# Tables of a state-space mixer with fewer instructions, B and C for eight groups at a time, phases by twos, and all pieces spread over the first feed forward

## The chip, the cores and the metric

The kernel runs on one core of a Trainium2 chip. The metric is the device time of one launch in microseconds (us); the median over runs is given. Engines are PE (TensorE, with its weight loads PEld), DVE (VectorE), ACT (ScalarE), POOL (GpSimd) and SP (SyncE, which here only issues DMAs). Each engine executes its instructions in the order in which they stand in its queue.

## The reference

A decoder trunk of two layers on x (1, 1024, 1024) in f32. Each layer is a mixer, a feed forward of squared ReLU (1024 to 4096 to 1024), and a gated per-layer embedding (PLE). Layer 0 mixes with RWKV-7 plus a short convolution, layer 1 with S5, a diagonal complex state space of 64 groups, with 16 channels and 64 states in each.

```python
def s5_mixer(hn, lambda_re, lambda_im, log_step, b_re, b_im, c_re, c_im, d_skip, glu_w1, glu_w2):
    u = hn.reshape(bsz, t, 64, 16)
    lam = complex(minimum(lambda_re, -1e-4), lambda_im)          # (64 groups, 64 states)
    step = exp(log_step)[:, None]
    lam_bar = exp(lam * step)
    b_bar = ((lam_bar - 1.0) / lam)[..., None] * complex(b_re, b_im)
    ...                                   # h[t] = lam_bar * h[t-1] + b_bar u[t];  y = Re(c h)
    y = gelu(y + d_skip * u)
    return (y @ glu_w1) * sigmoid(y @ glu_w2)

for i in range(2):
    h = h + mix_fns[i](rms_norm(h, norm_mix[i]), *mix_params[i])
    h = h + square(relu(rms_norm(h, norm_ffn[i]) @ ffn_up[i])) @ ffn_down[i]
    h = h + (p[i] @ ple_proj[i]) * sigmoid(rms_norm(h, norm_ple[i]) @ ple_gate[i])
return rms_norm(h, norm_final)
```

What the S5 mixer needs besides u depends on the parameters alone: powers of lam_bar, b_bar, its products with B and C, phases. None of it depends on x.

## The kernel before

The program runs through the mixer of layer 0, feed forward 0 (FFN0), PLE 0, S5 with its gated linear unit, feed forward 1 (FFN1), PLE 1 and the final norm. Every f32 product is made of three matmuls of a high and a low part (hi by hi, lo by hi, hi by lo: lines L159 to L161 in `mm3`).

**Feed forward** (`ffn`). A loop over k runs from -6 to 62; each k has 8 steps. In one k, PE executes 24 matmuls of the up projection into ps_up and 21 of the down projection, in seven groups of three into the three PSUM tiles ps_dnx, ps_dny and ps_dnz (L354); X is used by four of the seven. After each group, DVE adds the tile to h or ha (L357, "eviction"), and the next group on the same tile waits for that. The order of PE is written by hand (`manual_schedule`), and the table `due` says at which step an instruction of another engine, or of a piece, is emitted: `at(k, s, f)`. The order on the other engines is the scheduler's. For each k, DVE also makes r_up (L311, from PSUM), hidl (L319, the low part of an activation), a difference (L325) and the low part of the down weights wlo (L283); POOL makes the low part of the up weights (L260) and sums of down weights (L273 to L276), a quarter of the hidl and of the differences too. FFN0 and FFN1 execute the same matmuls of their own; only FFN0 has S5 work beside it.

The row norm for the feed forward comes through acc (POOL, L198, sums of squares), ps_ms (PE, L215), a reciprocal (DVE, L219) and ps_rs (PE, L225); L177 makes prl, the low part of the input of the up projection (16 of DVE).

**S5 work in FFN0.** `s5_tables` makes the tables of lam_bar by power series, on [128, 64] tiles on DVE (helpers `mul` L890, `add` L893, `sub` L896, `aff` L899). They are emitted before FFN0, and stand on DVE from 702 to about 900 us. After that come the pieces, one for 2 of the 64 groups, and the phases of a piece:

```python
S5_AT, S5_EACH, S5_FFN = 74, 8, 30
S5_STEPS = (0, 7, 8, 9, 10, 12, 13, 16, 18, 19), (9, 11, 13, 15, 17, 20)
for n, gs in enumerate(pieces(t5, range(S5_FFN))):
    for g, steps in zip(gs, S5_STEPS):
        for s in steps:
            at(0, S5_AT + S5_EACH * n + s, lambda g=g: next(g, 0))
```

So 30 of the 32 pieces begin at step 74 (k = 9) and follow each other by 8 steps, one in each k; the two others, with their phases, are woven into PLE 0. A piece (`s5_piece`) loads C and B of its 2 groups, turns C on PE (ps_c, L1049), scales it on DVE (cx, L1052), makes b_bar on DVE (u L1059, w L1060, o L1061, twice), CL on POOL (L1068 to L1071), BL on DVE (L1078, L1079, L1081), turns it on PE (ps_bl, L1087), makes the kernel block on PE (ps_k, L1095), and adds the skip block on POOL (L1099). `s5_phases` doubles a [128, 2, 128] table of phases in 7 steps, with two scalings on ACT and two operations on POOL (L1120, L1121) in a step.

**The end of mixer 0** (`mixer0_run`) is ordered by `MIX_JOBS`, one string for each chain of the recurrence; a job of `Wabc` is a part of the output projection (ps_wo) that fills PE while the chain waits. W45b, W67b read ybh and ybl (the convolution's half), W2b and W3b read yah and yal (the recurrence's half). `R` is the last step of the recurrence's read-out, `C6` and `C7` are steps of the convolution.

Of the kernel before, what the change touches and what calls it, by code (L numbers as in the profile page):

```python
# [5 lines left out]
F32 = mybir.dt.float32  # L6
# [6 lines left out]
P = 128  # L13
# [6 lines left out]
S5_AT, S5_EACH, S5_FFN = 74, 8, 30  # L20
S5_STEPS = (0, 7, 8, 9, 10, 12, 13, 16, 18, 19), (9, 11, 13, 15, 17, 20)
# [10 lines left out]
MIX_JOBS = ['z1 C0', 'z2 C1 W45a', 'z3 C2 X3', 'N M L z4 W01a', 'z5 C4', 'z6 W23a', 'z7 C5 S', 'W45b R C6', 'W01b C7', 'W67b W2b W3b', '']  # L32
# [25 lines left out]
class Trunk:  # L58
# [822 lines left out]
    def s5_tables(self, pool, sp, keep_p):  # L881
        nc, i = self.nc, self.i
        V = nc.vector
        n = [0]

        def t(nm="t"):
            return pool.tile([P, 64], F32, tag="s5t", name=nm, bufs=14)

        def mul(a, b):
            o = t(); V.tensor_mul(o, a, b); return o  # L890

        def add(a, b):
# [15 lines left out]
        def keep(a, nm, where=None):  # L908
            o = (where or pool).tile([P, 64], F32, name=nm); V.tensor_copy(o, a); return o

        def doub(E):
            return mul(E, aff(E, 1.0, 2.0))

        exp_c = [1.0 / m for m in range(2, 11)]

        def em1(x):
            return mul(horner(x, exp_c), x)

        def lam(nm):
# [7 lines left out]
        lre = pool.tile([P, 64], F32, name="lre")
        V.tensor_scalar_min(lre, lam("l1_lambda_re"), -1e-4)
        lim = pool.tile([P, 64], F32, name="lim")
        V.tensor_copy(lim, lam("l1_lambda_im"))  # L930
        ls = t("ls")
        nc.sync.dma_start(ls, i["l1_log_step"].rearrange("(o g) -> o g", o=1).broadcast_to([P, 64]))
        x = t("lsc")
        V.tensor_scalar(x, ls, -100.0, 1.0 / 128, ALU.max, ALU.mult)
        E = em1(x)
        for _ in range(4):
            E = doub(E)
        E = aff(E, 1.0, 1.0)
        for _ in range(3):
            E = mul(E, E)  # L940
        step = keep(E, "step")

        x = mul(lre, step)
        x2 = t("x2")
        V.tensor_scalar(x2, x, -80.0, 1.0 / 128, ALU.max, ALU.mult)
        E = em1(x2)
        for _ in range(7):
            E = doub(E)
        em = keep(E, "em")

        y = mul(lim, step)
        a = t("rnd")
        V.tensor_scalar(a, y, 1.0 / (2 * math.pi), 12582912.0, ALU.mult, ALU.add)
        nn = aff(a, 1.0, -12582912.0)
# [42 lines left out]
        m = mag  # L997
        for _ in range(3):
            m = mul(m, m)
        self.rho = keep_p.tile([P, 32], F32, name="rho")  # L1000
        for g in range(NG):
            V.tensor_copy(self.rho[64 * g:64 * g + 64], m.rearrange("p (q g) -> p g q", g=NG)[64 * g:64 * g + 64, g])

        raw = pool.tile([64, P], F32, tag="lraw", name="lraw", bufs=1)
        nc.sync.dma_start(raw.rearrange("g (r c) -> g r c", c=16),
                          i["l1_d_skip"].rearrange("(g o c) -> g o c", o=1, c=16).broadcast_to([64, 8, 16]))
        ps = self.pm.tile([P, H], F32, tag="m", name="ps_lam")
        nc.tensor.transpose(ps[:, 0:64], raw, self.ident[0:64, 0:64])
        eye = pool.tile([P, 16], F32, name="eye")
        V.tensor_reduce(eye, self.ident.rearrange("p (r c) -> p c r", c=16), mybir.AxisListType.X, ALU.add)  # L1010
        self.skip = sp.tile([P, 64, 16], F32, name="skip")
        V.tensor_copy(self.skip, ps[:, 0:64].rearrange("p (g o) -> p g o", o=1).broadcast_to([P, 64, 16]))
        V.tensor_mul(self.skip, self.skip, eye.rearrange("p (o c) -> p o c", o=1).broadcast_to([P, 64, 16]))


        r, im = cosy, siny
        self.wk = sp.tile([P, 7, 2, 32], F32, name="wk")
        for k in range(10):
            if k >= 3:
# [625 lines left out]
```

## Time and profile before

| | us |
|---|---|
| median of 3 runs (2765.99 to 2766.64) | 2766.43 |
| the profiled execution, its own time | 2769.96 |
| span of the profiled execution | 2768.2 |
| mixer 0, until 740.0 | 740.0 |
| FFN0, 740.0 to 1533.9 | 793.9 |
| PLE 0, 1533.9 to 1657.4 | 123.5 |
| FFN1, 1952.7 to 2628.6 | 675.9 |
| PLE 1, 2628.6 to 2751.8 | 123.2 |

The span is the time from the first to the last instruction; the profiled execution has 1.8 us around it, and is 3.5 us above the median. Times within the program are us from the start of the span. PE is busy for 94% of the span, DVE for 70%; the clock columns give the TensorE clock that was granted, as a share of 2.4 GHz.

### The profile page before, as it was taken

To read this page: it belongs to the slowest core of one execution; us is meant where nothing else is said; L and a number is where in the kernel's file an instruction comes from. 1 tells how busy PE (TensorE), PEld (TensorE's weight loads), DVE (VectorE), ACT (ScalarE), POOL (GpSimd) and SP (SyncE) were. 2 spreads that over 40 slices of the span, in tenths; PEclk is the share of its full clock that TensorE was granted. 3 is DMA by queue.
4 is the path that set the end of the run, shared out by engine and by line. 5 is a ranking of instruction groups with operands and counts; after the bars stand their busy time and mean duration, and the time that the engine had idled before them with its cause. 6 is when DMAs were issued, how large, how long until landed. Compare 5 with 4: busy or idle time off the path is not lost.

```text
span 2768.2 us, 48385 instructions
## 1 busy us (share of the span) xinstructions
PE 2601.9 (94%) x18829; PEld 2079.1 (75%) x18829; DVE 1928.5 (70%) x2992; ACT 1087.9 (39%) x2075; POOL 1178.5 (43%) x1771
## 2 busy tenths in 40 slices
PE   7999999989898889998999997899999999999998
PEld 5777777768676667777788786788788888888777
DVE  6655666563799888888777748622577777777854
ACT  4334444343432454444553525512433233233432
POOL 4434433443343577677663505511343433433410
PEclk9999999999899999999999998999999999999999
DMA  4213311321211233333211315311111111111121
GB/s 104 62 55 101 93 55 48 107 72 51 71 50 42 75 86 90 90 97 84 65 60 50 89 44 157 106 53 45 36 54 47 53 54 46 54 54 46 50 76 61
DMA packets 273441, 189.16 MB, mean 68 GB/s; under 512 B 36110, under 2 KB 255484, under 8 KB 273212
## 3 DMA queue, kind: packets, MB, share of 16 engines
q1 hardware_dynamic: 249232, 158.26, 19.5%
q10 hardware_dynamic: 21084, 19.17, 2.7%
q0 software_dynamic: 2896, 8.65, 0.9%
q8 instruction: 148, 2.42, 0.4%
q14 instruction: 81, 0.66, 0.1%
HBM read 156.92 MB, written 29.10 MB: 67 GB/s over the span
## 4 chain that ended last, share of the span: by engine, by line
PE 66%; DVE 14%; POOL 8%; issue 5%; DMA 3%; ACT 3%; SPq 0%; ACTq 0%; POOLq 0%; DVEq 0%
PE ps_dnx L354 9%; PE ps_up L161 6%; PE ps_up L159 6%; PE ps_up L160 6%; PE ps_dny L354 4%; PE ps_z L159 3%; PE ps_z L160 3%; PE ps_z L161 3%; PE ps_gl L159 2%; PE ps_gl L161 2%; PE ps_gl L160 2%; DVE ha L357 2%; PE ps_dnz L354 2%; PE ps_g L159 2%; PE ps_g L160 2%
## 5 line engine op out<-in xcount | busy, mean ns | idle before, releaser
L159 PE MATMUL ps_up<-prh,uwh 128*128 128x512 f32 x1024 | 407.6, 398 | 3.6 <-ACT uwh L257 3.6
L161 PE MATMUL ps_up<-prh,uwl 128*128 128x512 f32 x1024 | 408.5, 399 | 2.1 <-POOL uwl L260 2.1
L160 PE MATMUL ps_up<-prl,uwh 128*128 128x512 f32 x1024 | 406.0, 396 | 0.0
L260 POOL TENSOR_TENSOR uwl<-uraw,uwh 128x512 fp32r<-128x512 f32 x136 | 182.3, 1341 | 172.1 <-ACT uwh L257 171.2
L354 PE MATMUL ps_dnx<-hidh,whi 128*128 128x512 f32 x480 | 199.3, 415 | 46.4 <-DVE ha L357 46.1
L159 PEld LDWEIGHTS ps_up<-prh,uwh 128*128 128x128 f32 x1024 | 195.4, 191 | 49.5 <-ACT uwh L257 4.0
L161 PEld LDWEIGHTS ps_up<-prh,uwl 128*128 128x128 f32 x1024 | 194.9, 190 | 47.7 <-POOL uwl L260 2.6
L273 POOL TENSOR_TENSOR draw<-draw 128x128 f32<-128x128 f32 x120 | 65.3, 544 | 387.2 <-DMA draw<-in_l_ffn_down_dram 329.2
L160 PEld LDWEIGHTS ps_up<-prl,uwh 128*128 128x128 f32 x1024 | 195.1, 191 | 45.3
L148 POOL TENSOR_TENSOR wlo<-wraw,whi 128x1024 fp32r<-128x1024 f32 x66 | 159.6, 2420 | 141.7 <-ACT whi L147 129.2
L357 DVE TENSOR_TENSOR h<-h,ps_dnx 128x512 f32<-128x512 f32 x240 | 164.0, 683 | 57.5 <-PE ps_dnx L354 56.6
L198 POOL TENSOR_TENSOR acc<-acc,sq 128x512 f32<-128x512 f32 x70 | 104.8, 1505 | 215.3 <-ACT sq L197 214.5
L354 PE MATMUL ps_dnx<-hidl,whi 128*128 128x512 f32 x480 | 190.2, 396 | 4.5 <-DVE hidl L319 4.5
L354 PE MATMUL ps_dnx<-hidh,wlo 128*128 128x512 f32 x480 | 190.1, 396 | 0.0
L147 ACT CAST whi<-wraw 128x1024 fp32r<-128x1024 f32 x104 | 108.7, 1048 | 196.4 <-PE ps_z L160 73.2
L319 DVE TENSOR_TENSOR hidl<-r_up,hidh 128x512 fp32r<-128x512 f32 x188 | 158.8, 856 | 37.3 <-ACT r_up L315 30.8
L257 ACT CAST uwh<-uraw 128x512 fp32r<-128x512 f32 x136 | 84.0, 619 | 247.1 <-PE ps_up L160 234.0
L357 DVE TENSOR_TENSOR ha<-ha,ps_dnx 128x512 f32<-128x512 f32 x240 | 163.3, 680 | 18.4 <-PE ps_dnx L354 18.4
L159 PE MATMUL ps_z<-prh,whi 128*128 128x512 f32 x416 | 175.8, 423 | 0.1
L161 PE MATMUL ps_z<-prh,wlo 128*128 128x512 f32 x416 | 164.2, 395 | 1.7 <-POOL wlo L148 1.7
L160 PE MATMUL ps_z<-prl,whi 128*128 128x512 f32 x416 | 164.8, 396 | 0.6 <-DVE prl L480 0.6
L314 ACT ACTIVATE hidh<-r_up 128x512 fp32r<-128x512 f32 x98 | 61.7, 630 | 235.8 <-DVE r_up L311 228.9
(441 smaller groups left out, 6611.4 us busy)
## 6 DMA issues: line engine op xcount, KB each, us to landing
uraw<-in_l_ffn_up_dram SPq DMA_DIRECT2D x128, 256.0 KB
draw<-in_l_ffn_down_dram SPq DMA_DIRECT2D x120, 256.0 KB
wraw<-in_l_w_in_dram SPq DMA_DIRECT2D x52, 512.0 KB
s5w<-s5w SPq DMA_DIRECT2D x32, 384.0 KB
wraw<-in_l_w_out_dram SPq DMA_DIRECT2D x16, 512.0 KB
wraw<-in_l_ple_gate_dram SPq DMA_DIRECT2D x16, 512.0 KB
wraw<-in_l_glu_w_dram SPq DMA_DIRECT2D x16, 512.0 KB
toep<-kt ACTq DMA_DIRECT2D x32, 240.0 KB
```

The lines of the kernel that those rows point to most:

```text
L147: nc.scalar.copy(hi[:, :n], raw[:, :n])
L148: self.lo_engine().tensor_sub(lo[:, :n], raw[:, :n], hi[:, :n].bitcast(F32))
L159: nc.tensor.matmul(ps, wh, xh, start=start, stop=False)
L160: nc.tensor.matmul(ps, wh, xl, start=False, stop=False)
L161: nc.tensor.matmul(ps, wl, xh, start=False, stop=stop)
L198: (eng or nc.vector).tensor_add(acc, acc, sq)
L257: A.copy(uw[m][0], raws["u"])
L260: nc.gpsimd.tensor_sub(uw[m][1], raws["u"], uw[m][0].bitcast(F32))
L273: G.tensor_add(raw[:, 4], raw[:, 0], raw[:, 2])
L319: return lambda: eng.tensor_sub(st[nm][1], t, st[nm][0].bitcast(F32))
L354: nc.tensor.matmul(ps, w[:, a], v, start=id(ps) not in begun, stop=n == 2, skip_group_check=True)
L357: V.tensor_add(hv, hv, ps)
```

## The change

1. `s5_tables`: constants are folded into one instruction `(o + c) * x` (`series`) in place of a multiply and an affine one, tiles are written in place, powers of lam_bar are doubled (1, 2, 4 at a time) in place of one by one, and the phase factors wk lie in one tile `lv` and are copied by 2 instructions in place of 14. The 1024-wide skip table is gone: only its diagonal source dT and the mask eye16 are kept. DVE instructions of the tables: 272 before, 141 after. All loads of raw parameters are issued at the start. It is a generator now, called twice in each step from step -38 (in k = -5) on.
2. `s5_front` is new: loads, turns and scalings of B and C for 8 groups at once (8 fronts in place of 32 parts of pieces). The scaling of C moves from DVE to ACT; the skip product is made here on POOL, for 8 groups.
3. `s5_piece` keeps the rest: CL, BL, turn, kernel block.
4. `s5_phases` makes two pieces' phases in one call: the POOL instructions are half as many and twice as wide, the ACT instructions are as many as before.
5. The 32 pieces follow each other by 14 steps from step 36 to the end of FFN0; none is left for PLE 0.
6. `MIX_JOBS`: `W45b R C6` becomes `R C6 W45b`, `W67b W2b W3b` becomes `W2b W67b W3b`.

Lines from `s5_tables` on have other numbers in the changed kernel; those before it have 3 more.

```diff
-S5_AT, S5_EACH, S5_FFN = 74, 8, 30
-S5_STEPS = (0, 7, 8, 9, 10, 12, 13, 16, 18, 19), (9, 11, 13, 15, 17, 20)
+S5_START, S5_PREP, S5_AT, S5_EACH = -38, 2, 36, 14
+S5_FRONT = (-20, -6, -4, -3)
+S5_STEPS = (0, 2, 4, 7, 10)
+S5_PH = (1, 5, 9, 13, 17, 21, 25)
...
-MIX_JOBS = ['z1 C0', 'z2 C1 W45a', 'z3 C2 X3', 'N M L z4 W01a', 'z5 C4', 'z6 W23a', 'z7 C5 S', 'W45b R C6', 'W01b C7', 'W67b W2b W3b', '']
+MIX_JOBS = ['z1 C0', 'z2 C1 W45a', 'z3 C2 X3', 'N M L z4 W01a', 'z5 C4', 'z6 W23a', 'z7 C5 S', 'R C6 W45b', 'W01b C7', 'W2b W67b W3b', '']
...
-        def horner(x, coef):
-
-            p = aff(x, coef[-1], 1.0)
-            for c in reversed(coef[:-1]):
-                p = aff(mul(p, x), c, 1.0)
-            return p
...
+        def series(o, x, coef):
+
+            V.tensor_scalar_mul(o, x, float(coef[-1]))
+            for n, c in enumerate(reversed(coef[:-1])):
+                stt(o, o, float(c), x, ADD)
+                if n % 2:
+                    yield
...
-        for k in range(1, 8):
-            r, im, r1, i1 = self.LR[:, :, k], self.LI[:, :, k], self.LR[:, :, 1], self.LI[:, :, 1]
-            V.tensor_sub(self.LR[:, :, k + 1], mul(r, r1), mul(im, i1))
-            V.tensor_add(self.LI[:, :, k + 1], mul(r, i1), mul(im, r1))
...
+        for n in (1, 2, 4):
+            a, b = (q[:, :, 0:n] for q in tt)
+            lo, hi = slice(1, n + 1), slice(n + 1, 2 * n + 1)
+            rn, im = (q[:, :, n:n + 1].broadcast_to([P, 64, n]) for q in (R, I))
+            V.tensor_mul(a, R[:, :, lo], rn)
+            V.tensor_mul(b, I[:, :, lo], im)
+            yield
...
+    def s5_front(self, n, pool):
+        gs = slice(8 * n, 8 * n + 8)
...
+        ps = self.pm.tile([P, H], F32, tag="m", name="ps_c")
+        for m, raw in enumerate(raws):
+            nc.tensor.transpose(ps[:, m * P:(m + 1) * P], raw, self.ident)
+        X = pool.tile([P, 2, 8, 16], F32, tag="cx", name="cx", bufs=1)
+        nc.scalar.activation(X.rearrange("p n g c -> p (n g c)"), ps[:, 0:2 * P], AF.Copy, scale=self.nsgn)
+        yield
+        bc = lambda a: a.rearrange("p (g o) -> p g o", o=1).broadcast_to([P, 8, 16])
...
+        for m in range(2):
+            V.tensor_mul(Bb[:, m], Bs[m], bc(self.Fr[:, gs]))
+            V.tensor_mul(w, Bs[1 - m], bc(self.Fi[:, m, gs]))
+            V.tensor_add(Bb[:, m], Bb[:, m], w)
...
+            for j in range(2):
+                for o, n in ((E[:, j, :, m:2 * m], 0), (t[:, j, :, :m], 1)):
+                    nc.scalar.activation(o, E[:, j, :, 0:m], AF.Copy, scale=self.wk[:, k, n, pc + j:pc + j + 1])
+            G.tensor_sub(E[:, :, 0, m:2 * m], E[:, :, 0, m:2 * m], t[:, :, 1, :m])
+            G.tensor_add(E[:, :, 1, m:2 * m], E[:, :, 1, m:2 * m], t[:, :, 0, :m])
...
+                            def start(s):
+                                for _ in range(S5_PREP):
+                                    if next(tab, self) is self:
+                                        return
+                                at(0, s + 1, lambda: start(s + 1))
+                            at(0, S5_START, lambda: start(S5_START))
+                            for n in range(64 // NG):
+                                s0 = S5_AT + S5_EACH * n
+                                gs = [(lazy(self.s5_piece, n), S5_STEPS)]
...
-                            side = pieces(t5, range(S5_FFN, 64 // NG))
-                        self.ple(l, st2["xn"], rstd, pt, done1, [q for a, b in side for q in [a] * 4 + [b] + [a, b] * 5 + [a]])
+                        self.ple(l, st2["xn"], rstd, pt, done1, [])
```

**PE, the end of mixer 0.** These are rows of PE behind the last step of the recurrence (ps_z is a last part of the input projection, ps_yt turns the recurrence's result). Before, the 48 ybh and ybl matmuls come first:

```order
L161 MATMUL ps_z<-prh,wlo 128x512
L159 MATMUL ps_wo<-ybh,whi 128x512
L160 MATMUL ps_wo<-ybl,whi 128x512
L161 MATMUL ps_wo<-ybh,wlo 128x512
L159 MATMUL ps_wo<-ybh,whi 128x512
...
L799 MATMUL ps_yt<-ident,Y 128x128 x4
L159 MATMUL ps_wo<-yah,whi 128x512
```

After, 24 matmuls of the other half stand at this place, and ybh only behind them:

```order
L164 MATMUL ps_z<-prh,wlo 128x512
L162 MATMUL ps_wo<-yah,whi 128x512
L163 MATMUL ps_wo<-yal,whi 128x512
L164 MATMUL ps_wo<-yah,wlo 128x512
...
L162 MATMUL ps_wo<-ybh,whi 128x512
L163 MATMUL ps_wo<-ybl,whi 128x512
...
L802 MATMUL ps_yt<-ident,Y 128x128 x4
L162 MATMUL ps_wo<-ybh,whi 128x512
```

So 24 matmuls that read earlier results moved ahead of the first ones that need the second half of ybh; as many of the ybh ones moved behind ps_yt.

**PE, the start of FFN0.** These rows are those around ps_ms and ps_rs, through which the row norm passes. Before, 28 matmuls of ps_up stand ahead of ps_ms and 21 between it and ps_rs:

```order
L159 MATMUL ps_up<-prh,uwh 128x512
L215 MATMUL ps_ms<-meanw,acc 128x1 x4
L160 MATMUL ps_up<-prl,uwh 128x512
L161 MATMUL ps_up<-prh,uwl 128x512
...
L159 MATMUL ps_up<-prh,uwh 128x512
L225 MATMUL ps_rs<-ident,rs_8946 128x128 x4
L924 MATMUL ps_lam<-ident,lraw 128x64
L160 MATMUL ps_up<-prl,uwh 128x512
```

After, 9 of ps_up stand ahead of ps_ms, and none between ps_ms, ps_rs and the three ps_lam of the tables:

```order
L164 MATMUL ps_up<-prh,uwl 128x512
L218 MATMUL ps_ms<-meanw,acc 128x1 x4
L228 MATMUL ps_rs<-ident,rs_8946 128x128 x4
L915 MATMUL ps_lam<-ident,lraw_l_lambda_re 128x64
L915 MATMUL ps_lam<-ident,lraw_l_lambda_im 128x64
L915 MATMUL ps_lam<-ident,lraw_d 128x64
L162 MATMUL ps_up<-prh,uwh 128x512
L163 MATMUL ps_up<-prl,uwh 128x512
```

40 matmuls of ps_up moved from before ps_rs to behind it.

**DVE, the start of FFN0.** Here are the rows from the reciprocal of the row norm on. Before, two of the tables stand between it and the first r_up:

```order
L177 SCALAR_TENSOR_TENSOR prl<-ha_8854,cv_359,prh 128x512
L219 RECIPROCAL rs_8946<-sd_8944 128x4
L928 TENSOR_SCALAR lre<-ps_lam 128x64
L890 TENSOR_TENSOR t<-lre,step 128x64
L311 SCALAR_TENSOR_TENSOR r_up<-ps_up,rstd 128x512
L945 TENSOR_SCALAR x_9065<-t 128x64
L311 SCALAR_TENSOR_TENSOR r_up<-ps_up,rstd 128x512
L899 TENSOR_SCALAR t<-x_9065 128x64
L890 TENSOR_TENSOR t<-t,x_9065 128x64
```

After, 68 instructions of the tables stand between the reciprocal and the first r_up, and 15, 26 and 9 more ahead of the second, third and fourth; up to the fourth hidl they are 121:

```order
L222 RECIPROCAL rs_8946<-sd_8944 128x4
L927 TENSOR_SCALAR lre<-ps_lam 128x64
L951 TENSOR_TENSOR x<-lre,step 128x64
L997 TENSOR_TENSOR u_9174<-lre 128x64
...
L1034 TENSOR_TENSOR tt_9232<-LI 128x64
L314 SCALAR_TENSOR_TENSOR r_up<-ps_up,rstd 128x512
L1043 TENSOR_TENSOR mag<-mag 128x64
L1056 TENSOR_TENSOR sq<-rj 128x128
```

So most of the tables, which before stood among the instructions of the first nine k, moved ahead of the first r_up or between the first few; besides the 121 of them, ten instructions of the feed forward stand between the reciprocal and the fourth hidl (four r_up, three hidl, two differences, one wlo).

## Rows read from the trace of the kernel before

**Rows 1.** The page's busy time, share of the span and instructions by engine.

```profile
PE 2601.9 (94%) x18829; PEld 2079.1 (75%) x18829; DVE 1928.5 (70%) x2992; ACT 1087.9 (39%) x2075; POOL 1178.5 (43%) x1771
```

**Rows 2.** Windows: from:to, us, busy PE PEld DVE ACT POOL (instructions), clock, DMA share.

```profile
699.10:736.40 37.30, 29.28 (x103) 20.83 (x101) 30.45 (x67) 11.26 (x19) 9.69 (x5) 0.86 0.28 94
740.00:782.80 42.80, 37.37 (x153) 28.80 (x153) 38.28 (x67) 19.62 (x33) 21.59 (x19) 0.92 0.18 51
782.80:893.60 110.80, 100.32 (x407) 78.39 (x408) 107.64 (x271) 30.18 (x44) 37.18 (x51) 0.96 0.14 43
893.60:1319.90 426.30, 384.44 (x1681) 301.11 (x1680) 373.58 (x694) 203.33 (x537) 299.83 (x654) 0.96 0.33 87
1319.90:1488.80 168.90, 167.85 (x721) 134.85 (x720) 128.33 (x182) 81.67 (x202) 101.46 (x241) 1.00 0.20 59
782.80:1533.90 751.10, 697.01 (x3000) 550.41 (x3001) 646.68 (x1194) 336.80 (x818) 458.42 (x963) 0.97 0.26 72
1988.00:2628.60 640.60, 638.27 (x2760) 518.40 (x2761) 493.95 (x693) 207.01 (x308) 253.23 (x335) 1.00 0.17 51
```

**Rows 3.** Waits of PE, 893.6 to 1319.9: us in total, times, longest.

```profile
PE ps_dnx L354 <- DVE ha L357: 34.7, 23, 3.8
PE ps_c L1049 <- DMA craw<-in_l_c_im_dram: 5.7, 1, 5.7
```

**Rows 4.** Timeline of PE around a piece: start, us, line, tile, count.

```profile
1001.13 0.38 PE L1087 MATMUL ps_bl<-ident,BL 128*128 128x128 f32 x2
1001.27 0.49 PE L354 MATMUL ps_dny<-hidh,whi 128*128 128x512 f32 x1
...
1002.06 0.61 PE L1095 MATMUL ps_k<-CL,brep 128*128 128x128 f32 x4
1002.43 0.47 PE L354 MATMUL ps_dnx<-hidh,whi 128*128 128x512 f32 x1
```

**Rows 5.** Groups by line, DVE, 893 to 1320: busy us, mean ns, idle before.

```profile
L1078 DVE TENSOR_TENSOR BL<-LR,o 128x256 f32<-128x256 f32 x30 | 31.1, 1038 | 0.0
...
L1060 DVE TENSOR_TENSOR w<-bx,Fi 128x32 f32<-128x32 f32 x60 | 19.4, 324 | 0.3 <-DMA bx<-in_l_b_re_dram 0.3
L1059 DVE TENSOR_TENSOR u<-bx,Fr 128x32 f32<-128x32 f32 x60 | 19.2, 320 | 1.9 <-DMA bx<-in_l_b_im_dram 1.0
L1079 DVE TENSOR_TENSOR tmp<-LI,o 128x256 f32<-128x256 f32 x30 | 15.7, 525 | 1.3 <-POOL CL L1071 1.1
L1061 DVE TENSOR_TENSOR o<-u,w 128x32 f32<-128x32 f32 x60 | 13.7, 228 | 1.0
L1081 DVE TENSOR_TENSOR BL<-BL,tmp 128x256 f32<-128x256 f32 x30 | 13.3, 442 | 0.1
L1052 DVE TENSOR_SCALAR cx<-ps_c,signs 128x64 f32<-128x64 f32 x30 | 8.2, 273 | 3.8 <-PE ps_c L1049 3.8
```

**Rows 6.** Timeline of PE at the start of FFN0, idle time before in brackets.

```profile
751.50 0.95 PE L215 MATMUL ps_ms<-meanw,acc 128*128 128x1 f32 x8
...
757.28 1.05 PE L225 MATMUL ps_rs<-ident,rs 128*128 128x128 f32 x8
...
782.79 0.80 PE L354 MATMUL ps_dnx<-hidl,whi 128*128 128x512 f32 x1 [3.28 <-DVE hidl L319]
```

**Rows 7.** Timeline of DVE at the start of FFN0.

```profile
755.31 0.17 DVE L219 RECIPROCAL rs<-sd 128x4 f32<-128x4 f32 x1
...
759.07 0.69 DVE L311 SCALAR_TENSOR_TENSOR r_up<-ps_up,rstd 128x512 f32<-128x512 f32 x1
```

**Rows 8.** Groups by line, DVE, 756 to 772.

```profile
L890 DVE TENSOR_TENSOR t<-t,x 128x64 f32<-128x64 f32 x9 | 2.0, 224 | 0.3
L890 DVE TENSOR_TENSOR t<-t 128x64 f32<-128x64 f32 x3 | 1.6, 541 | 0.1
```

**Rows 9.** Waits of PE, 699 to 760.

```profile
PE ps_wo L159 <- ACT ybh L817: 5.2, 1, 5.2
```

**Rows 10.** Waits of PE, 577.5 to 653.7.

```profile
PE ps_wo L159 <- ACT ybh L817: 6.3, 1, 6.3
```

More of the change, by code (lines that the diff above doesn't have):

```diff
@@ L925, in lam @@
             return ps[:, 0:64]
[L927 to L937, printed above, removed]
@@ L938, in s5_tables @@
-        E = aff(E, 1.0, 1.0)
-        for _ in range(3):
[L940 to L954, printed above, removed]
+        raws = [lam("l1_lambda_re"), lam("l1_lambda_im")]
@@ new lines, in s5_tables @@
+        yield
+        self.dT = t("dT", where=sp)
+        V.tensor_copy(self.dT, turned(raws[2]))
+        self.eye16 = t("eye16", (16,), sp)
+        V.tensor_reduce(self.eye16, self.ident.rearrange("p (r c) -> p c r", c=16), mybir.AxisListType.X, ADD)
+        yield
+        fact = lambda n: math.factorial(n)
+        exp_c = [1.0 / fact(m) for m in range(1, 11)]
+        x, E = t("x"), t("E")
+        ts(x, step, -100.0, 1.0 / 128, MAX, MUL)
+        yield from series(E, x, exp_c)
+        for n in range(4):
+            stt(E, E, 2.0, E, ADD)
+            if n % 2:
+                yield
@@ new lines, in s5_tables @@
+        ts(step, E, 1.0, 1.0)
+        for _ in range(3):
+            V.tensor_mul(step, step, step)
+        yield
+        em = E
+        V.tensor_mul(x, lre, step)
+        ts(x, x, -80.0, 1.0 / 128, MAX, MUL)
+        yield from series(em, x, exp_c)
+        for n in range(7):
+            stt(em, em, 2.0, em, ADD)
+            if n % 2:
+                yield
+        y, nn = t("y"), t("nn")
+        V.tensor_mul(y, lim, step)
+        ts(nn, y, 1.0 / (2 * math.pi), 12582912.0)
+        yield
@@ L997, in s5_tables @@
-        m = mag
+            stt(y, nn, -float(cc), y, MUL, ADD)
+        yield
+        hq = nn
+        ts(y, y, 0.5, 0.0)
+        V.tensor_mul(hq, y, y)
+        yield
+        sn, cn = t("sn"), t("cn")
+        yield from series(sn, hq, [(-1.0) ** m / fact(2 * m + 1) for m in range(1, 8)])
+        stt(sn, sn, 1.0, y, ADD)
+        yield from series(cn, hq, [(-1.0) ** m / fact(2 * m) for m in range(1, 9)])
+        ts(cn, cn, 1.0, 1.0)
+        yield
+        ri, cm1, mag = t("ri", (2, 64)), t("cm1"), t("mag")
@@ new lines, in s5_tables @@
+        V.tensor_add(u, u, w)
+        yield
+        V.reciprocal(inv, u)
+        self.Fr = t("Fr", where=sp)
+        V.tensor_mul(u, nr, lre)
+        yield
+        V.tensor_mul(w, ni, lim)
+        V.tensor_add(u, u, w)
+        yield
+        V.tensor_mul(self.Fr, u, inv)
+        self.Fi = t("Fi", (2, 64), sp)
+        V.tensor_mul(u, ni, lre)
+        yield
+        V.tensor_mul(w, nr, lim)
+        V.tensor_sub(u, u, w)
+        yield
+        sgn = self.sgn
+        stt(self.Fi[:, 0], u, sgn, inv, MUL)
@@ L1016, in s5_tables @@
[L1016 to L1019, printed above, removed]
[L1020 to L1025 removed]
+            V.tensor_copy(self.rho[64 * g:64 * g + 64], mag.rearrange("p (q g) -> p g q", g=NG)[64 * g:64 * g + 64, g])
@@ new lines, in s5_tables @@
+        yield
+        self.wk = t("wk", (7, 2, 32), sp)
+        lv = t("lv", (7, 2, 64))
+        sq, rj = t("sq", (2, 64)), t("rj", (2, 64))
+        for k in range(9):
+            o = lv[:, k - 2] if k >= 2 else (rj, ri)[k]
+            V.tensor_mul(sq, ri, ri)
+            V.tensor_sub(o[:, 0], sq[:, 0], sq[:, 1])
+            stt(o[:, 1], ri[:, 0], 2.0, ri[:, 1], MUL)
+            ri = o
+            yield
+        for g in range(NG):
+            V.tensor_copy(self.wk[64 * g:64 * g + 64].rearrange("p k n q -> p (k n) q"),
+                          lv.rearrange("p k n (q g) -> p g (k n) q", g=NG)[64 * g:64 * g + 64, g])
@@ new lines, in s5_front, with s5_piece @@
+        self.eight = X, Bb, sk
+        yield
+    def s5_piece(self, pc, pool):
+        nc = self.nc
+        g0 = pc * NG
+        gs, q = slice(g0, g0 + NG), slice(g0 % 8, g0 % 8 + NG)
+        G = nc.gpsimd
+        V = nc.vector
+        big = lambda nm: pool.tile([P, NG, 9, 16], F32, tag="s5b", name=nm, bufs=4)
+        bcc = lambda ap, k: ap.rearrange("p g (k o) -> p g k o", o=1).broadcast_to([P, NG, k, 16])
+        bck = lambda t, k: t.rearrange("p g (o c) -> p g o c", o=1).broadcast_to([P, NG, k, 16])
+        X, Bb, sk = self.eight
+        X, Bb = [X[:, n, q] for n in range(2)], [Bb[:, n, q] for n in range(2)]
```

211 lines of the change are left out of this document (95 added, 116 removed).

## The prediction, made before the changed kernel was run

> **What bounds the kernel now.** I read the busy times first: PE works for 94% of the span, DVE for 70% [rows 1]. As an average this says that PE sets the time. The windows then say where it does not [rows 2]. FFN1 is the measure: 2760 matmuls in 640.6 us, 638.27 of them busy, at full clock, so 0.2321 us per matmul, and this with DVE at 493.95 / 640.6 = 77%. FFN0 from the same point of its program on (the second matmul of its third down group) needs 751.1 us. That is **110.5 us more**, and it is where the S5 work lies. Taken by stretch, with 0.2321 for each matmul that is FFN0's own:
>
> - 782.8 to 893.6, tables on DVE: 110.8 - 407 x 0.2321 = +16.3. DVE is busy for 107.64 of 110.8 us.
> - 893.6 to 1319.9, the 30 pieces: 240 of the 1681 matmuls belong to pieces (8 each); 426.3 - 1441 x 0.2321 = +91.8, or 3.06 for each piece.
> - 1319.9 to 1488.8, phases only: 168.9 - 721 x 0.2321 = +1.6. ACT and POOL work beside the feed forward costs almost nothing here, with DVE at 128.33 / 168.9 = 76%.
>
> What the 3.06 are made of is in the waits of PE in that stretch: 34.7 us for the eviction L357 on DVE, in 23 waits, and 5.7 for one late load of C [rows 3]. The granted clock of 0.96 over 426.3 us adds about 0.04 x 426.3 = 17. The rest is PE's own work on pieces. So this stretch is paced by DVE. One k is 45 matmuls, 10.4 us at FFN1's rate, and has 0.771 x 10.4 = 8.05 us of DVE. A piece adds 4.02 us of DVE: the seven groups sum to 120.6 us for 30 [rows 5]. That is 12.1 us of DVE in a k, against 11.3 of PE with the piece's matmuls (0.8, below): 107%.
>
> **The change, part by part.** The sum is made against the profiled execution, 2769.96 us, and then carried to the median, which is 3.5 lower.
>
> *A. Pieces and tables in FFN0, from the point above on.* A piece keeps on PE the turn (1001.13 to 1001.27, 0.14 us) and the kernel block (1002.06 to 1002.43, 0.37) [rows 4]. The turn of C had two small matmuls in every piece, which I put at 0.3 by estimate (twice the pair above), 0.8 for the whole piece; it becomes one pair of 128x128 turns for four pieces, 0.14 by the pair of the same shape. So 32 x 0.51 + 8 x 0.14 = 17.4 us of PE work stays. On DVE a piece keeps BL, tmp and their sum, (31.1 + 15.7 + 13.3) / 30 = 2.0 us [rows 5]. The six front operations of 128x128 have no row; they lie between 32 wide (0.23 to 0.32) and 256 wide (0.44 to 1.04). I take 0.4 each, 2.4 per front, 0.6 per piece. So 2.6 in 14 steps, which are 1.75 k: 14.1 + 2.6 = 16.7 us of DVE against 18.3 + 0.5 = 18.8 of PE, **89%**. At 77% nothing waits (FFN1), at 107% a piece costs (34.7 + 5.7 + 17) / 30 = 1.9 us in waits and clock. In a straight line 89% would cost 0.76; I take **0.6** a piece, 19 us, as queues that have slack recover between pieces. Bounds: 0 (the phases stretch) and 1.9, 61 us (before's price kept). The tables stand at the start now, so the +16.3 of the first stretch is gone from here and is paid for in B. A is 17.4 + 19 - 110.5 = **-74.1**.
>
> The scaling of C on ACT and the skip product on POOL have no row either. They cost nothing to the end as long as both engines have slack: ACT was busy for 203.33 of 426.3 us, POOL for 299.83 (70%), with a piece in every k. With 1.75 k for a piece POOL falls to below that even if the twice as wide phases save nothing. Should POOL be late, its hidl and differences are late next, then the down groups.
>
> *B. The start of FFN0.* In the changed order ps_ms stands behind 9 matmuls of ps_up, and ps_rs at once behind it. Before, ps_ms ran at 751.50 and ps_rs at 757.28 [rows 6], under cover of 49 matmuls. The reciprocal between them ended at 755.5 [rows 7], behind sixteen prl, and those don't move. So PE idles until about 755.5, and 40 matmuls, 9.3 us, stand behind it. DVE is later still. Behind the reciprocal 68 table instructions precede the first r_up (at 759.07 before), and 121 precede the fourth hidl. At 0.224 for a 64-wide one alone [rows 8], with the wider ones of the doubling, I take 0.27 on average: 32.7 us. The four r_up take 4 x 0.69 [rows 7], the other six feed forward instructions about 0.9 each by estimate: 40.9 us from 755.5, so 796.4. The matmul that ran at 782.79, after a wait of 3.28 for its hidl [rows 6], comes one hidl later, at about 799.5: +16.7, and +1.3 for a half clock behind the idle time. B is **+18**. Bounds: +6 (only the 9.3 us of PE, less the 3.28 that waited anyway) and +40 (below).
>
> *C. The end of mixer 0.* PE is busy for 29.28 of 37.3 us there, at a clock of 0.86 [rows 2]; 5.2 of the idle time is a wait for ybh [rows 9]. Now 24 matmuls that need only earlier results, 5.6 us, stand at that place. That removes the wait, and most of the half clock behind it, 0.14 x 37.3 = 5.2 us. DVE, 30.45 of 37.3, limits what is gained, although it loses half of its table instructions there. I take **-9**, bounds -5 (the wait alone) and -13.
>
> *D. W45b behind R and C6.* PE waits 6.3 us for ybh in that stage [rows 10]. That goes, but the recurrence's next step then runs without filler. I take **-4**, bounds -8 and +6.
>
> *E. PLE 0* loses two pieces: two times 0.8 of PE, **-1**; PLE 0 (123.5) and PLE 1 (123.2) differ by 0.3.
>
> Sum: -74.1 + 18 - 9 - 4 - 1 = **-70.1**. The profiled execution would be 2699.9, the median 2766.43 - 70.1 = **2696**.
>
> **The rivals.**
>
> *R1, DVE still paces the pieces.* The waits and the half clocks stay as they were for each piece, 61 us in place of 19: 2738. For it: bursts count, not shares, and BL alone holds DVE for 1.04 us. Against it: each piece brings two thirds of its DVE work, and 1.75 times as rarely.
>
> *R2, everything hides.* No wait is left in the pieces (-19), and the start costs PE's 6 only (-12): 2665. For it: the phases stretch at 76%. Against it: the tables are on DVE ahead of r_up whatever PE does.
>
> *R3, it gets slower.* A piece's DVE operations are late at ps_bl and ps_k. PE's order is fixed, and ps_bl stands only 3 steps (3.9 us) behind the emission of the last BL operation, so PE waits with everything behind it. If each of 32 pieces waited 2.5 us, with 1.7 of half clock behind it: 134 in place of 19, 2811. It decides from 89 / 32 = 2.8 us a piece. Against it: before, the distance was 3 steps too, with a fuller DVE, and no wait for BL stands among PE's waits [rows 3].
>
> *R4, the table instructions at the start run beside POOL.* The same multiply of 64 columns took 0.224 us in nine cases and 0.541 on average in three others, within 16 us [rows 8]. At the higher price the 68 instructions ahead of r_up take 68 x 0.32 = 22 us more, the start costs +40, the time is 2718. For it: POOL makes uwl and sums of draw there. Against it: nine of twelve ran at the low price.
>
> The Trainium skill (SBUF — State Buffer, Who interferes with whom) has a rule beside R4: the second input of a DVE instruction that reads two operands from SBUF comes through an interface shared with GpSimd, and an exclusive lock makes one of them wait. By that rule the change trades affine instructions with one such operand, which the page exempts outside the two-port modes, for two-input ones, and R4's 2718 would be the time if POOL were reading throughout. The trace agrees as far as two prices for one instruction go.
>
> **How the numbers follow.** Forecast 0.54, R1 0.17, R2 0.11, R4 0.11, R3 0.07. The likeliest gives 2696; its own range, with C, D and half of B's bounds, is 2683 to 2711. The range for all is **2662 to 2740**: it takes in R1, R2 and R4, and leaves out R3 and the ends where bad values meet. A difference under 0.2% (5.5 us) can't be told from none here. R1 with B at +40 ends at 2760, near that; I give 0.03 to the same, 0.06 to slower (R3 above its point), 0.91 to faster.
>
> **What would show it.** Right: from its third down group on FFN0 takes about 677 us, in place of 751.1, with DVE near 89% and L357 waits under 15 us in all; the first r_up stands near 775; no idle time ahead of the ybh matmuls in the tail. A: wrong if waits for L357 are again over 1 us a piece, or waits for BL or CL appear at ps_bl and ps_k. B: wrong if the third down group comes before 790 or after 810. C, D: wrong if the mixer ends later than 733 or earlier than 720. Most of the forecast hangs on A; a front whose operations take twice my price would bring DVE to 92% and not undo it, but a wait on the fixed order of PE would.

## The result and the profile after

The changed kernel takes 2728.49 us (median of 4 runs, 2723.54 to 2734.85), the kernel before 2766.21 in the same comparison: a ratio of 0.9867, with an interval of 0.9844 to 0.9891. It is 1.3% faster. The range held it (2662 to 2740) and the sign was right, but the gain is 38 us where 70 were forecast. The profiled execution is the fastest of its four, 2723.54 us with a span of 2721.8, so it stands 46.4 below the one of before. These 46.4 are more than the gain: the profiled execution of before lies 3.8 above its median and this one 5.0 below, so the parts together are 8.7 too large. The parts of the 46.4:

| part | forecast | before | after | measured |
|---|---|---|---|---|
| A: FFN0 from the second matmul of its third down group on | -74.1 | 751.1 | 710.4 | -40.7 |
| B: first ps_up to that matmul | +18 | 42.8 | 54.8 | +12.0 |
| C and D: mixer 0, until the first ps_up | -13 | 740.0 | 725.4 | -14.6 |
| E: PLE 0 | -1 | 123.5 | 119.5 | -4.0 |
| S5 and gated unit (1657.4 to 1952.7; 1610.1 to 1904.8) | 0 | 295.3 | 294.7 | -0.6 |

What is left (+1.5) lies in FFN1 and behind it. Part A is uncertain by the most: the kernel before with nothing but the new jobs (below), whose rows of PE in this stretch are those of before, took 743.1 us for it where before took 751.1, so A is a gain of 33 to 41 us. Here are windows of the changed kernel: from and to, us, busy time of PE, PEld, DVE, ACT, POOL, then clock, DMA share and GB/s. They answer to [rows 2].

```profile
690.00:725.40 35.40, 27.42 (x124) 19.50 (x118) 32.58 (x57) 15.33 (x26) 13.18 (x10) 1.00 0.31 101
725.40:780.20 54.80, 41.52 (x152) 31.62 (x152) 49.54 (x154) 20.93 (x41) 24.76 (x24) 0.78 0.15 39
780.20:1490.60 710.40, 674.54 (x2967) 537.83 (x2967) 572.55 (x836) 335.04 (x852) 430.19 (x751) 1.00 0.28 78
1490.60:1610.10 119.50, 117.47 (x531) 95.44 (x530) 65.16 (x84) 39.62 (x59) 11.39 (x11) 1.00 0.19 58
1940.00:2580.50 640.50, 638.17 (x2760) 517.79 (x2761) 494.38 (x693) 206.89 (x308) 253.55 (x335) 1.00 0.17 51
```

FFN0 is still 70 us longer than FFN1, with DVE at 572.55 / 710.40 = 81%, further from full than before (86%), and POOL at 61% as before. The clock hardly takes part any more (1.00, rounded). The waits of PE in that window answer to [rows 3]:

```profile
PE ps_dnx L357 <- DVE ha L360: 28.2, 30, 2.3
PE ps_dnx L357 <- DVE h L360: 6.7, 5, 2.0
PE ps_dnx L357 <- DVE hidl L322: 1.7, 1, 1.7
PE ps_k L1146 <- ACT bi L1140: 0.5, 1, 0.5
```

The eviction (now L360) is still what ends them: 34.9 us, as before with 30 pieces (34.7). The next two views show what makes an eviction late on a DVE that has a fifth of its time free. First, the waits of DVE itself, 836 to 1490. It waits for PE when it has nothing to do, which costs nothing; the third and fourth rows are others:

```profile
DVE h L360 <- PE ps_dnx L357: 29.2, 37, 1.4
DVE ha L360 <- PE ps_dny L357: 24.1, 16, 2.1
DVE hidl L322 <- ACT r_up L318: 15.2, 12, 3.7
DVE BL L1129 <- POOL CL L1123: 12.8, 10, 2.3
```

For 28 us DVE stands before an instruction that ACT or POOL has not released. BL does not read CL; what it must wait for is a buffer, that of an input of CL's sum (tag s5b, 4 buffers for 6 tiles). hidl waits for a square on ACT, and ACT stands in its own queue before the phases, which wait for POOL. Here are ACT's waits in the same window:

```profile
ACT phase L1170 <- POOL phase L1172: 38.4, 39, 2.9
...
ACT phase L1170 <- POOL phase L1164: 19.1, 5, 6.8
```

Second, DVE's groups by line, 836 to 1490: busy us, mean ns, idle before. They answer to [rows 5].

```profile
L360 DVE TENSOR_TENSOR h<-h,ps_dnx 128x512 f32<-128x512 f32 x110 | 75.1, 682 | 29.7 <-PE ps_dnx L357 29.2
...
L322 DVE TENSOR_TENSOR hidl<-r_up,hidh 128x512 fp32r<-128x512 f32 x81 | 70.2, 879 | 18.7 <-ACT r_up L318 15.2 <-ACT hidh L330 2.2
...
L328 DVE TENSOR_TENSOR r_up<-r_up 128x512 f32<-128x512 f32 x38 | 35.5, 935 | 2.4 <-ACT r_up L318 2.2
L1129 DVE TENSOR_TENSOR BL<-LR,Bb 128x256 f32<-128x256 f32 x31 | 24.7, 797 | 13.3 <-POOL CL L1123 12.8 <-PE ps_k L1146 0.4
L1132 DVE TENSOR_TENSOR BL<-BL,tmp 128x256 f32<-128x256 f32 x31 | 20.0, 646 | 0.2
L1130 DVE TENSOR_TENSOR tmp<-LI,Bb 128x256 f32<-128x256 f32 x31 | 18.1, 584 | 0.4 <-DMA s5w<-bi 0.3
L1096 DVE TENSOR_TENSOR Bb<-Bb,w 128x128 f32<-128x128 f32 x14 | 5.4, 384 | 0.1
```

The eviction, with one input in PSUM, never varies. In the two-input ones the mean stands above the shortest: 0.80 against 0.41 us for L1129, 0.88 against 0.67 for hidl. I call the sum of (duration less that of the shortest tenth of the group) the stretch: it is 67 us here and 25 in the same stretch of FFN1, where only the feed forward's own POOL work runs. The Trainium skill (SBUF — State Buffer, Who interferes with whom) names such a contention; the trace agrees in which instructions are hit. Of the 265 two-input operations of BL, hidl, r_up (L328) and wlo in this stretch, 117 took at least a tenth longer than the shortest of their line, and each of these had a POOL instruction beside it. Of the 69 without one, none took more than 4% longer. The 384 evictions had POOL beside them for 61% of their time and none was stretched.

One late eviction shows the two together. Here DVE waits 1.8 us for CL's sum, BL then takes 1.50 us in place of 0.41, and three evictions stand behind the three operations of BL; PE waits 2.0 us for the last of them:

```profile
1200.54 1.50 DVE L1129 TENSOR_TENSOR BL<-LR,Bb 128x256 f32<-128x256 f32 x1 [1.78 <-POOL CL L1123]
...
1202.81 0.68 DVE L360 TENSOR_TENSOR ha<-ha,ps_dny 128x512 f32<-128x512 f32 x1
1203.40 0.68 DVE L360 TENSOR_TENSOR h<-h,ps_dnx 128x512 f32<-128x512 f32 x1
1204.00 0.68 DVE L360 TENSOR_TENSOR ha<-ha,ps_dnx 128x512 f32<-128x512 f32 x1
...
1204.83 0.47 PE L357 MATMUL ps_dnx<-hidh,whi 128*128 128x512 f32 x1 [2.01 <-DVE ha L360]
```

From each of the 35 evictions that PE waited for, one can follow DVE back to its last idle time over 0.1 us. In 26 cases ACT or POOL ended that idle time (26.5 of the 35 us that PE waited), in 5 PE, in 4 a DMA; in 22 of the 26 the work between it and the eviction holds 0.5 us or more of stretch. Of the 383 evictions that PE did not wait for, ACT or POOL stand behind 144, or 38%.

### The profile page after: what moved, and what is told of

The parts are those of the page before. It is cut to its first block, busy times and chain, and to the rows that moved or that the text cites. A ratio compares the mean times of both kernels' runs of the same rounds, so it can differ in the third digit from the quotient of the medians.

```text
span 2721.8 us, 47184 instructions
## 1 busy us (share of the span) xinstructions
PE 2571.1 (94%) x18781; PEld 2058.4 (76%) x18781; DVE 1860.5 (68%) x2685; ACT 1078.4 (40%) x2083; POOL 1140.2 (42%) x1524
## 4 chain that ended last, share of the span: by engine, by line
PE 67%; DVE 13%; POOL 7%; issue 5%; ACT 4%; DMA 4%; SPq 0%; ACTq 0%; POOLq 0%; DVEq 0%
PE ps_dnx L357 9%; PE ps_up L164 6%; PE ps_up L162 6%; PE ps_up L163 6%; PE ps_dny L357 4%; PE ps_z L162 3%; PE ps_z L163 3%; PE ps_z L164 2%; PE ps_gl L162 2%; PE ps_gl L163 2%; PE ps_gl L164 2%; PE ps_g L164 2%; PE ps_g L162 2%; PE ps_g L163 2%; PE ps_dnz L357 2%
## 5 line engine op out<-in xcount | busy, mean ns | idle before, releaser
L357 PE MATMUL ps_dnx<-hidh,whi 128*128 128x512 f32 x480 | 196.8, 410 | 37.1 <-DVE ha L360 28.2
L360 DVE TENSOR_TENSOR h<-h,ps_dnx 128x512 f32<-128x512 f32 x240 | 164.1, 684 | 72.1 <-PE ps_dnx L357 71.2
L357 PE MATMUL ps_dnx<-hidl,whi 128*128 128x512 f32 x480 | 188.8, 393 | 2.8 <-DVE hidl L322 2.8
L357 PE MATMUL ps_dnx<-hidh,wlo 128*128 128x512 f32 x480 | 189.0, 394 | 0.3 <-DVE wlo L286 0.3
L360 DVE TENSOR_TENSOR ha<-ha,ps_dnx 128x512 f32<-128x512 f32 x240 | 163.5, 681 | 22.4 <-PE ps_dnx L357 22.2
L322 DVE TENSOR_TENSOR hidl<-r_up,hidh 128x512 fp32r<-128x512 f32 x188 | 152.0, 821 | 27.3 <-ACT r_up L318 20.3
```

The lines of the kernel that those rows point to most:

```text
L322: return lambda: eng.tensor_sub(st[nm][1], t, st[nm][0].bitcast(F32))
L357: nc.tensor.matmul(ps, w[:, a], v, start=id(ps) not in begun, stop=n == 2, skip_group_check=True)
L360: V.tensor_add(hv, hv, ps)
```

## The experiments

The forecast held that slack on DVE decides (DVE LOAD). Against it stand STRETCH (called POOL at first: two-input operations last longer beside POOL), and HEAD OF QUEUE (DVE waits in order for ACT or POOL). The measure is the window from the second matmul of the third down group to FFN0's end, in the profiled execution: 710.4 us in the changed kernel, 640.5 in FFN1. Two of the kernels below turned out to have the changed kernel's instructions in its order on every engine; they repeat it, with windows of 714.9 and 709.6 and medians of 2731.69 and 2725.66. So differences under some 5 us in the window mean nothing. The diffs are cut to the lines that matter, and what stands behind # in them is a remark.

**Pieces emitted behind FFN0 (e1).**

```diff
-                            for n in range(64 // NG):
+                            for n in range(0):
...
                         self.ffn(l, st["xn"], st["rstd"], done2, hook)
+                    for n in range(64 // NG): ...   # front, piece, phases, all steps at once
```

> All fronts, pieces and phases run between FFN0 and PLE 0 in place of beside FFN0; the tables stay at the start of FFN0. If the pieces are what costs FFN0 its 70 us over FFN1, FFN0 from the second matmul of its third down group on takes 640 to 648 us (710.3 with the pieces beside it). If something of the start (tables, norm) still trails behind, it stays above 655. The start itself, from the first ps_up to that matmul, 54.8 us in the changed kernel, stays within 2 us of that by both. The whole is slower than the changed kernel by what the 32 pieces cost in a row: some 150 to 200 us less 65, so 2790 to 2860.

Measured: 2726.08 us, as the changed kernel, and a window of 708.5. The edit did not do what it says. The pieces' instructions stood behind FFN0 in the code, but the trace shows them beside it, packed into its first half:

```profile
793.00:1153.00 360.00, 333.50 (x1464) 267.44 (x1463) 296.92 (x452) 205.38 (x607) 283.22 (x527) 0.96 0.37 100
1153.00:1489.00 336.00, 334.69 (x1449) 271.62 (x1448) 261.31 (x364) 123.60 (x223) 142.26 (x207) 1.00 0.18 54
```

By accident it is a test of the spacing: 32 pieces at 11.3 us apiece cost together what they cost at 20 us apiece, although 0.04 x 360 = 14 us of the dense sum go with the granted clock of 0.96. The spread over all of FFN0 gained nothing beyond the noise.

**Phases emitted behind FFN0 (e2).**

```diff
-                                if n % 2 == 0:
+                                if False:
                                     gs.append((lazy(self.s5_phases, n), S5_PH))
...
+                    for n in range(0, 64 // NG, 2): ...   # all steps of the phases
```

> Only the phases move behind FFN0; pieces and fronts stay beside it. Theory POOL (two-input operations of DVE are stretched while POOL reads, and then evictions come late): POOL loses about a fifth of its work there, the stretch of DVE's operations over their shortest falls from 67 us in the changed kernel to 50 or less, and FFN0 from the third down group on falls from 710 to 685-697. Theory DVE LOAD (the piece's own DVE work falls into the eviction's place): DVE's work is as before, so 705 to 712. The whole is slower by what the phases cost in a row behind FFN0, some 60 to 90 us.

Measured: 2731.69, window 714.9. The phases were moved back to where they had been: the order is that of the changed kernel, row for row on each engine. It is the first of the two repeats and tells nothing of either theory.

**BL on POOL (e3).**

```diff
-        V.tensor_mul(BL[:, :, 0:8], bcc(LR[:, :, 0:8], 8), bck(Bb[0], 8))
+        G.tensor_mul(BL[:, :, 0:8], bcc(LR[:, :, 0:8], 8), bck(Bb[0], 8))
```

(the same for its second product and the sum)

> The three operations of a piece that make BL move from DVE to POOL. Theory DVE LOAD: only the fronts are left on DVE, FFN0 from the third down group on falls from 710 to 665-680, the whole to about 2690. Theory POOL: DVE loses 2.0 us a piece but POOL reads 2.4 us more a piece, hidl, r_up and wlo are stretched more, 685 to 705, the whole 2705 to 2722. A third way: POOL becomes late for its own hidl and uwl, waits for POOL appear on PE, over 710.

Measured: 2711.53 us, ratio to before 0.981 (0.9794 to 0.9826), so faster than the changed kernel too; its interval lies below that one's. The window is 695.9, against 665 to 680 for DVE LOAD and 685 to 705 for STRETCH. DVE lost 33 us of busy time there and the time fell by 14.5; the stretch stayed at 65, since hidl, r_up and wlo took it over (r_up at a mean of 1103 ns). BL's wait for CL left DVE with it, so the gain does not single out STRETCH.

**Tables from step -24 (e4).**

```diff
-S5_START, S5_PREP, S5_AT, S5_EACH = -38, 2, 36, 14
+S5_START, S5_PREP, S5_AT, S5_EACH = -24, 2, 36, 14
```

> The tables' first call comes 14 steps later, so that 48 in place of 9 matmuls of ps_up stand ahead of the norm's ps_ms and ps_rs. Theory ORDER OF PE (the start is later because ps_ms and ps_rs stand too early): the waits of 4.7 and 1.7 us go, the half clock of 20 us there too, and the start falls from 54.8 to 42-48 us, the whole by 7 to 12. Theory TABLES (it is later because 121 table instructions stand on DVE ahead of the fourth hidl): the start stays at 52 to 58.

Measured: the start falls from 54.8 to 46.6 us, and PE's waits at ps_ms and ps_rs are gone. But the edit moved two things. On PE 28 matmuls of ps_up stand ahead of ps_ms in place of 9 (48 were expected). On DVE one table instruction stands between the reciprocal and the first r_up in place of 68, and 74 rows between it and the fourth hidl in place of 131:

```profile
742.22 0.16 DVE L222 RECIPROCAL rs<-sd 128x4 f32<-128x4 f32 x1
745.93 0.23 DVE L927 TENSOR_SCALAR lre<-ps_lam 128x64 f32<-128x64 f32 x1 [3.54 <-PE ps_lam L915]
746.07 1.28 DVE L314 SCALAR_TENSOR_TENSOR r_up<-ps_up,rstd 128x512 f32<-128x512 f32 x2
```

So 8 of the 12 us of B hang on where the tables start; this run does not tell the order on PE from the tables on DVE. The window grew to 716.3, and the whole is 2723.5 (ratio 0.984 to 0.987), which can't be told from the changed kernel.

**One phase table (e5); one CL (e6); one BL (e7).** Three kernels leave work out: phases for all but the first pair, CL for all but the first piece, BL for all but the first piece.

```diff
-        for k in range(7):
+        E = self.E0                      # made for pc == 0 alone
+        for k in range(7 if pc == 0 else 0):
...
-        CL, tmp = big("CL"), big("tmp")
+        CL = self.CL0                    # made for pc == 0 alone; big has 3 buffers
...
-        BL, tmp = big("BL"), big("tmp3")
+        BL = self.BL0                    # made for pc == 0 alone; big has 3 buffers
```

> Left out: the phases of all pieces but the first pair, whose table is written for all (the DMAs stay). POOL loses about 62 of its 391 us in the pieces' stretch, ACT its 28 scalings a pair. Theory POOL (two-input operations of DVE are stretched while POOL reads): the stretch over the shortest falls from 67 to about 55 us and FFN0 from the third down group on from 710 to 696-704. Theory DVE LOAD: 707 to 716. If ACT's or POOL's queue behind the phases were what is late, it would fall further, under 690.

> Left out: CL of all pieces but the first, which is used for all; 78 us of POOL's longest operations of a piece go. DVE does what it did. Theory POOL: the stretch falls from 67 to 50 or less, FFN0 from the third down group on from 710 to 690-700. Theory DVE LOAD: 707 to 716.

> Left out: BL of all pieces but the first, which is used for all. DVE loses 39 us at the shortest price and 24 us of stretch; POOL does what it did (BL on POOL in place of DVE left 695.9). Theory DVE LOAD: 672 to 685. Theory POOL: hidl, r_up and wlo are still stretched by CL and phases, 688 to 698.

Measured: windows of 705.1, 693.2 and 706.0; medians of 2719.81, 2708.78 and 2720.39; stretch 62, 54 and 52. Taking CL off POOL, with DVE's work untouched, is worth 17 us. One phase table is worth more than its window says. With nothing to compute, POOL issues the transfers of all phase tables at the start, and sums of draw stand among them:

```profile
799.84 4.25 POOL L1182 DMA_DIRECT2D s5w<-phase  x8
...
806.18 5.87 POOL L1182 DMA_DIRECT2D s5w<-phase  x11
812.06 0.47 POOL L278 TENSOR_TENSOR draw<-draw 128x128 f32<-128x128 f32 x1
...
817.90 0.79 PE L357 MATMUL ps_dnx<-hidh,whi 128*128 128x512 f32 x1 [6.67 <-ACT whi L283]
```

(from e12, where it is the same). Counted from a matmul behind this stall to FFN0's end, one phase table takes 56 us more than FFN1 for the same matmuls, one CL 52, the changed kernel 69 (its repeats 73 and 68). With one phase table hidl's wait for ACT falls from 15.2 to 3.0 us (836 to 1487). Taking BL off DVE, 41 us of its busy time, is worth 4, which is within the repeats. That is the opposite of DVE LOAD. STRETCH does not fit e7 either (688 to 698): its stretch fell as it should, the time did not. What did grow in it are DVE's waits for ACT, 23.8 us for hidl in place of 15.2. The smaller number of buffers in e6 and e7 is a second change beside the work left out, and may have a part in that: in e6 DVE waits 7.8 us for the transfer of bi, which it hardly did before (0.3).

**The kernel before with the new jobs (e8).**

```diff
-MIX_JOBS = [..., 'W45b R C6', 'W01b C7', 'W67b W2b W3b', '']
+MIX_JOBS = [..., 'R C6 W45b', 'W01b C7', 'W2b W67b W3b', '']
```

> The kernel before with only the two strings of the mixer's jobs changed. The mixer's end (first ps_up of FFN0) moves from 740.0 to 725-728 as in the changed kernel (725.4), FFN0 and the rest keep their lengths, and the whole falls by 12 to 15 us to about 2752. If part of the 14.6 us at this place came from the tables' shorter row of DVE in the tail, it falls by 5 to 10 only.

Measured: 2755.94, a ratio of 0.9967 (0.9956 to 0.9977). The first ps_up is at 733.2: the jobs are worth about 6.8 of the 14.6 us (one execution each; in the eleven other kernels with the changed end of mixer 0 the first ps_up lies between 724.8 and 728.9). In the tail 24 matmuls now stand where PE waited, but the next wait is for DVE:

```profile
PE ps_wo L159 <- DVE cv L564: 3.9, 1, 3.9
```

The other 7.8 us come with the rest of the change, in which fewer table instructions stand on DVE there; that was not tried by itself.

**Emission steps of BL and of the phases (e9, e10, e11).** Three kernels that leave nothing out; e11 has both edits, and the tables from step -24.

```diff
-S5_STEPS = (0, 2, 4, 7, 10)
-S5_PH = (1, 5, 9, 13, 17, 21, 25)
+S5_STEPS = (0, 2, 4, 6, 9, 12)                 # e9, e11: a yield between CL's sum and BL
+S5_PH = (0, 2, 5, 8, 11, 15, 19, 23, 26)       # e10, e11: memset and each doubling by itself
```

> A yield between the sum of CL on POOL and the products of BL on DVE, and steps 0, 2, 4, 6, 9, 12: BL is emitted two steps behind that sum, whose input tile is the buffer that BL takes. No work is left out. Theory HEAD OF QUEUE (DVE stands before an instruction that waits for POOL or ACT, and the evictions behind it come late): the waits of DVE for CL ahead of BL, 12.8 us in the changed kernel, fall to under 4, and FFN0 from the third down group on falls from 710 to 698-706. Theory STRETCH (two-input operations last longer beside POOL, no matter who waits): no change, 707 to 716.

> The memset and the first two doublings of a pair of phases are emitted at steps of their own (9 parts in place of 7). No work is left out. Theory HEAD OF QUEUE: ACT's waits for POOL in the phases (38.4 and, for the memset, 19.1 us) fall by a third or more, DVE's hidl waits less for r_up of ACT (15.2 us), and FFN0 from the third down group on falls by 4 to 10 us from 710. Theory STRETCH: no change, 707 to 716.

> Both of these edits and the tables from step -24. By HEAD OF QUEUE the gains add: FFN0 from the third down group on 690 to 702, the start 46 to 48, the whole 2700 to 2712. By STRETCH only the start's 8 us are left, less what the pieces' stretch gave back when the tables started later (6 us of 8): 2720 to 2727.

Measured: windows of 714.8, 709.6 and 717.0; medians of 2723.41, 2725.66 and 2721.2. The phases' nine parts (e10) changed no row of the order on any engine; it is the second repeat. In e9 BL stands three rows later on DVE, and its wait for CL fell from 12.8 to 8.4 us, but hidl's wait for ACT rose from 15.2 to 22.2: one wait for another. So HEAD OF QUEUE was hardly put to the test by these, and is neither shown nor refuted by them. In e11 the start is again 46 us and the window again longer, as in e4; the whole lies where STRETCH had put it (2720 to 2727), which says little, as the phases did not move.

**Both left out on POOL and ACT (e12).** The edits of the phases and of CL together.

> Left out: both the phases (all but the first pair's) and CL (all but the first piece's); DVE keeps all of its work for pieces, 14 steps apart. FFN0 from the third down group on would be 657 with PE's own 17 us for pieces alone; the changed kernel has 710, CL alone left out gave 693, phases alone 705. Theory POOL AND ACT (what makes evictions late is the pieces' work on POOL and ACT, through stretched two-input operations and through instructions of DVE that wait for them): the gains add, 675 to 688, and the stretch of DVE's operations falls below 48 us. Theory DVE LOAD (the piece's own 2.6 us on DVE in bursts): a floor of about 690 stays, 689 to 696.

Measured: 2703.33 us, window 686.6, within the range of POOL AND ACT and below that of DVE LOAD; both gains add. DVE has all its work, and the two waits are almost gone:

```profile
PE ps_dnx L357 <- DVE h L360: 5.9, 5, 1.9
PE ps_dnx L357 <- DVE ha L360: 4.2, 9, 0.9
...
DVE hidl L322 <- ACT r_up L318: 3.8, 6, 1.8
```

(the first two of PE, the third of DVE, 836 to 1480). The stretch to FFN0's end was 48, the bound that was expected. Of 15 late evictions 4 follow an idle time of DVE that ACT or POOL ended (3.1 of the 10.4 us), where it was 26 of 35. From 846.0 to the end the kernel takes 37 us more than FFN1 for the same matmuls, the changed kernel 69 from the same matmul on. PE's own work for pieces is 17 of these: what is left is 20 us, or 0.63 for a piece, where the changed kernel has 52 and 1.6. At the start of the pieces this kernel, like the one with one phase table, has the stall of 6.7 us that the others lack: sums of draw on POOL came late, whi on ACT behind them, then a down group. Over the whole window, stall included, 29 us are left of 53.

## Why the prediction was right or wrong

**A failed in one term.** PE's work for pieces was 17.4 by forecast and about 17 in the trace (0.14 and 0.36 for each piece, 0.14 for each front). DVE's work was right too: 16.4 us in 14 steps, 16.7 by forecast (836 to 1490 holds 2738 matmuls, 210 of them of pieces, so 78.75 take 654.0 x 78.75 / 2528 = 20.4 us, of which DVE works 527.58 / 654.0). The front's six operations took 0.34 to 0.38, at a price of 0.4. What failed is the price of waiting: 0.6 a piece, 19 us, from DVE's share between two rows. It measured 53 us, 1.65 a piece; the waits for L357 alone are 34.9 / 32 = 1.1 us a piece, over the 1 us that the prediction had set as the sign of being wrong. The step was "ACT and POOL cost nothing to the end as long as both have slack". They have slack (46% and 60% busy), and still three fifths of the waits are theirs, counted behind the stall: with CL and phases gone DVE is as busy (81%) and a piece costs 0.63, near the 0.6 that I had taken for DVE's load alone. Nor does a share explain e1: by the forecast's straight line the dense pieces (DVE at about 100%) would cost some 46 us and the spread ones 24; they measured 51 and 53 (windows of 708.5 and 710.4, less 640.5 and 17).

How the 1 us a piece divides between stretched operations and DVE's waits for ACT and POOL stays open: both stand ahead of most late evictions. One BL alone lowered the first and not the time; the edits that aimed at the second did not reach it. That the range held the result is owed to its width, which took in R1, not to A.

**R1** (the old price of waiting stays, 2738) was nearest, at a chance of 0.17, with R4's 2718 about as near by accident. Of R1's reason one half stands, that shares do not decide. But its mechanism, DVE pacing the pieces by its own work, is not what was found. **R2** is refuted. **R3** did not come: PE waits 0.5 us at ps_k and nothing at ps_bl. No row gave its 1.7 us of half clock behind a wait, nor the +1.3 in B; the waits of up to 2.3 us in the pieces left the clock at 1.00. **R4** is refuted where I put it: the 68 table instructions ahead of the first r_up took about 13 us (753.09 against ps_rs at 740.03), below even the 0.27 each of the forecast. Two-input operations that last longer beside POOL come further on, in the pieces.

**B** (+18, measured +12): the mechanism fits, though no run tests it by itself. PE waits 1.7 us at ps_ms and 4.7 at ps_rs, as foreseen, and 1.7 for a hidl in the end, so DVE's row ended last; the table instructions were priced too high. The granted clock of 0.78 over these 54.8 us, for which 1.3 us stood in the sum, need not add to it, since PE waited for DVE in the end. The fourth hidl ended 50.7 us behind the first ps_up, 56.4 by forecast. **C and D** (-13, measured -14.6): the size is right, the reason half so. The jobs give about 6.8. **E** (-1, measured -4.0) fell by more than PE's work for two pieces; of the 4.0, 2.3 are PE's (119.79 us before, 117.47 after).

## What to carry to other kernels

An engine with a fifth of its time free can still be late for its neighbour at every turn, when its queue is in order and what stands ahead of the urgent instruction waits for a slower engine. Before pricing work on such engines at nothing, list what the engine ahead of the bottleneck waits for, and which buffers a new instruction takes over. And check in a trace that work moved in the source has moved on the engine: here two edits left every row where it was.

## What the runs showed of the hardware

The same two-input operation of DVE on 128x256 took 0.41 to 1.58 us beside POOL's work, while evictions from PSUM stayed within 0.67 to 0.70 in all runs, 840 in each. Repeated waits of up to 2.3 us left the granted clock at 1.00 (rounded) over 710 us, while the start of FFN0, with waits of 3.6, 2.2, 1.7 and 4.7 us within 19 us, ran at 0.78, where it had been 0.92. A DMA issue on POOL held its queue for about 0.53 us (8 in 4.25, 11 in 5.87).
